# Gathering expert tokens with the hidden state as the stationary operand

## The chip, the cores and the metric

The kernel runs on one core of a Trainium2 chip. The metric is the device time of one execution in microseconds (us), the median of several runs. TensorE is the matmul engine (PE in the profile; PEld is its loading of the stationary operand), VectorE is DVE, ScalarE is ACT, GpSimd is POOL, and SP is the queue that issues the transfers from HBM.

## What is computed

Two layers of a transformer trunk over 256 tokens of width 1024. The second layer's channel mixer is a mixture of experts, and the change lies there:

```python
logits = xf @ w_router                       # 256 x 8
top_logits, top_e = top_k(logits, 2)
gates = softmax(top_logits)
...
y = swiglu(x[rows of expert e], w1[e], w3[e], w2[e])   # for each of 8 experts
out[token] += y[row] * gate[row]
```

All weights are float32; the eight experts alone have 352 MB of them, each read once.

## The kernel before, in words

**Stages.** Layer 0 ends near 410 us of the profiled span, the attention of layer 1 near 570 us, the experts run from about 590 to 1470 us, and the last gate projection closes the kernel. Matrix products with the large experts and dense layers are made of three passes over numbers split in two: `hi` is the value rounded to the chip's single-pass float32 form (float32r, written by ACT), `lo` is the rest (written by DVE). `mm3` (lines 141 to 144) multiplies hi by hi, lo by hi, hi by lo. `split_unit` (lines 93 to 112) splits 1024 columns of weights at a time: `whi` on ACT (line 103), `wlo` on DVE (line 111); five buffers of each.

**Weights.** SP issues transfers of 1 MB into rings of twelve raw buffers (`raw`, `side`, `post`, `early`), in the program's order; a buffer is free again once its weights have been split or, for the small experts, multiplied.

**Router.** `norm_turn` (lines 403 to 428) normalises h, transposes it (line 280), splits the transposed halves (lines 137 and 138) and has the router's matmuls made (lines 460, 461). Then `swiglu_moe` copies the logits (`lgT`, line 997), turns them (line 1000), finds the two best experts of each token (lines 1008, 1009), builds the one-hot choice (lines 1012 to 1017) and each token's slot in its expert's list (lines 1021 to 1025), and counts (line 1028). Lines 1031 to 1033 split h itself, in its natural layout with tokens on the partitions, into `hsh` (ACT, line 137) and `hsl` (DVE, line 138), 128x1024 for each of the two tiles of tokens. `gates()` and `ranks()` (lines 1044 to 1089) make the gate values and sort the experts by their count; line 1088 reads the sorted experts' numbers into SP's registers, and every later transfer of a sorted expert's weights needs them.

**Gather.** For each expert, `gather` (lines 1096 to 1145) builds a one-hot matrix `oh` (tokens x places, line 1103), multiplies it as the stationary operand by hsh and hsl as the moving ones (lines 1116, 1117: eight matmuls of 512 columns, two tiles of tokens, two halves of the width, hi and lo), copies the sums to `xs` (ACT, line 1118), transposes `xs` in eight pieces (line 1131 for a large expert, line 1123 for a small one), and copies or splits the result into the form in which it is a stationary operand itself: `xg_h`, `xg_l` (lines 137, 138) for a large expert, `xe` (line 1124) for a small one. Then `oh` is transposed for the way back (line 1138), and the gate of each row is gathered (line 1140). Five experts have 128 places (large), one 64 and two 32 (small).

**Order.** `STEPS` lists 26 (expert, columns) steps by hand. Expert 0 is gathered first, two steps are done with it, and each other expert is gathered two steps ahead of its first step. Within that, the framework's scheduler orders the instructions of each engine: an instruction traced earlier goes first if it is ready; `tc.issue_after(x)` puts the instructions traced in its block behind x, but only those on x's own engine. In the profiled run the eight gathers begin on PE at 592.0 (expert 0), 609.3 (rank 7, 32 places), 725.2 (rank 1), 890.3 (rank 2), 940.8 (rank 5, 64 places), 1096.7 (rank 3), 1156.1 (rank 6, 32 places) and 1266.2 us (rank 4).

Of the kernel before, what the change touches and what calls it, by code (L numbers as in the profile page):

```python
# [9 lines left out]
FT = mybir.dt.float32  # L10
# [4 lines left out]
AF = mybir.ActivationFunctionType  # L15
# [3 lines left out]
S, D, DEPTH = 256, 1024, 2  # L19
NT = S // 128  # L20
KD = D // 128
N_IN = 2956
D_FF, N_EXP = 3584, 8
# [30 lines left out]
def body(ctx, tc, nc, I, out):  # L54
# [5 lines left out]
    def ps_tile(shape, tag, bufs):  # L60
        return psum.tile(shape, FT, tag=tag, name=tag, bufs=bufs)
# [4 lines left out]
    def work():  # L66
        return ps_tile([128, 512], "wk", 4)
# [22 lines left out]
    last = {}  # L90
# [45 lines left out]
    def split_sb(hi, lo, src):  # L136
        ins = nc.scalar.activation(hi, src, AF.Copy)
        last["lo"] = nc.vector.tensor_sub(lo, src, hi.bitcast(FT))  # L138
        return ins
# [12 lines left out]
    ident = consts.tile([128, 128], FT, name="ident")  # L152
    nc.vector.tensor_scalar(ident, rel, 0.0, None, op0=OP.is_equal)
    h = pers.tile([128, NT, D], FT, name="h")
# [832 lines left out]
    def swiglu_moe(hT, logits, closing):  # L987
        hh, hl = hT
        with tc.tile_pool(name="moe", bufs=1, reuse_waits="tile") as mp:
            hsh = mp.tile([128, NT, D], FR, name="hsh")  # L990
            hsl = mp.tile([128, NT, D], FR, name="hsl")
            sums = pers.tile([128, NT, 2], FT, name="sums", tag="lnsm", bufs=2)
            quarters = mp.tile([128, NT, 4], FT, name="quarters")
            table("exp_and_others", last["sqrt"])
            lgT = mp.tile([128, D], FT, name="lgT", tag="xs", bufs=1)[:2 * N_EXP, :S]
            for t in range(NT):
                nc.vector.tensor_copy(lgT[:, t * 128:(t + 1) * 128], logits[t])
            ps = work()[:, :NT * 2 * N_EXP].rearrange("p (t j e) -> p t j e", t=NT, j=2)
# [31 lines left out]
            done = {}  # L1030
            with tc.issue_after(last["turn"].ins):
                for t in range(NT):
                    done["hs"] = split_sb(hsh[:, t], hsl[:, t], h[:, t])
            xg_h = pers.tile([128, KD, 256], FR, name="xgh", tag="hTh")
            xg_l = pers.tile([128, KD, 256], FR, name="xgl", tag="hTl")

# [59 lines left out]
            def gather(r, n, off, half):  # L1096


                small = n < 128
                sr, gr = (slot, gate) if r == 0 else (slot_r, gate_r)  # L1100
                oh = mp.tile([128, NT, 128], FR, name="oh", tag="oh", bufs=1)
                for t in range(NT):
                    done["oh"] = nc.vector.tensor_scalar(
                        oh[:, t].rearrange("p (j s) -> p j s", s=n),
                        slots[:, None, off:off + n].to_broadcast([128, 128 // n, n]),
                        sr[:, t, r:r + 1], None, op0=OP.is_equal)
                if off == 0 and r == 0:
                    with tc.issue_after(done["oh"].ins):
                        gates()
                        ranks()  # L1110
                xs = mp.tile([128, D], FT, name="xs", tag="xs", bufs=1)
                for f in range(2):
                    fs = slice(f * 512, (f + 1) * 512)
                    p = work()
                    for t in range(NT):
                        nc.tensor.matmul(p, oh[:, t], hsh[:, t, fs], start=t == 0, stop=False)
                        nc.tensor.matmul(p, oh[:, t], hsl[:, t, fs], start=False, stop=t == NT - 1)
                    nc.scalar.activation(xs[:, fs], p, AF.Copy)
                if small:
                    x = mp.tile([128, KD, 64], FT, name="xe", tag="xe", bufs=1)[:, :, :n]  # L1120
                    p = work()[:, :KD * n].rearrange("p (a b) -> p a b", b=n)
                    for k in range(KD):
                        nc.tensor.transpose(p[:, k], xs[:n, k * 128:(k + 1) * 128], ident[:n, :n])
                    nc.scalar.activation(x, p, AF.Copy)
                else:
                    b0 = half * 128
                    x = xg_h[:, :, b0:b0 + 128], xg_l[:, :, b0:b0 + 128]
                    for k0 in range(0, KD, 4):
                        p = work().rearrange("p (a b) -> p a b", a=4)
                        for j in range(4):  # L1130
                            nc.tensor.transpose(p[:, j], xs[:, (k0 + j) * 128:(k0 + j + 1) * 128], ident)
                        ins = split_sb(x[0][:, k0:k0 + 4], x[1][:, k0:k0 + 4], p)
                    if off == 0 and r == 0:
                        table("silu_and_others", ins)
                p = work()
                ohT = mp.tile([128, NT, 128], FR, name="ohT", tag="ohT", bufs=3)
                for t in range(NT):
                    nc.tensor.transpose(p[:, t * 128:(t + 1) * 128], oh[:, t].bitcast(FT), ident)
                for t in range(NT):
                    nc.tensor.matmul(p[:, 256:257], oh[:, t].bitcast(FT), gr[:, t, r:r + 1],  # L1140
                                     start=t == 0, stop=t == NT - 1)
                nc.scalar.activation(ohT, p[:, :256].rearrange("p (t b) -> p t b", t=NT), AF.Copy)
                gs = mp.tile([128, 1], FT, name="gs", tag="gs", bufs=3)
                nc.vector.tensor_copy(gs, p[:, 256:257])
                return x, ohT, gs
# [333 lines left out]
```

## Time and profile before

| | |
|---|---|
| median of 3 runs | 1513.24 us (1512.91 to 1515.36) |
| the profiled execution | 1511.99 us, its span 1510.2 us |
| PE busy | 1421.4 us (94%) |
| weight loads (PEld) | 1054.7 us (70%) |
| DVE busy | 975.8 us (65%) |
| ACT busy | 812.8 us (54%) |
| read from HBM | 454.42 MB, 302 GB/s over the span |

In the timeline a row gives the start in us, the duration in us, the engine, the line, the operation, the result and its inputs, the tile's shape, the number of instructions merged (x4: the duration is then from the first start to the last end), and in brackets the idle time before it with what ended it. A matmul's duration is longer than the distance to the next one, since matmuls are pipelined; the distance from start to start is what one costs. In the table of stretches the columns are the stretch, its length, busy us of each engine with the count of instructions, the granted clock of TensorE as a share of 2.4 GHz, the busy share of the DMA engines, and GB/s.

### The profile page before, as it was taken

Reading aid. Unit: us, or ns where it says so; the run is one execution under the profiler, and the core shown is the slowest. Engines: PE = TensorE matmul, PEld = TensorE weight load, DVE = VectorE, ACT = ScalarE, POOL = GpSimd, SP = SyncE. Lnnn points to the kernel's source line nnn. Section 1 sums busy time; section 2 is a strip of 40 time slices with the busy share of each in tenths; the row PEclk is TensorE's granted clock in tenths of the full one; section 3 lists DMA queues with packets and bytes.
Section 4 is the critical chain, followed back from the end, with each engine's and each line's share of the span. In section 5 each row is a group of like instructions: output and inputs, shape, how many; then the busy total and the mean of one; then the engine's idle time right before and its main releaser. Section 6 shows DMA issues by size and latency. Waiting matters only on the chain. (4 is left out here: it accounts for less than half of the span.)

```text
span 1510.2 us, 19841 instructions
## 1 busy us (share of the span) xinstructions
PE 1421.4 (94%) x7298; PEld 1054.7 (70%) x7298; DVE 975.8 (65%) x1347; ACT 812.8 (54%) x1120; POOL 8.1 (1%) x16
## 2 busy tenths in 40 slices
PE   7999899999999997988999989999899997999968
PEld 6677788888786776746877668853478755777736
DVE  7676654554676767626888568930288854898745
ACT  5466543443555466526766457720277644777534
POOL 0000000000000000000000000000000000000000
PEclk9999999999999998999999999999999999999989
DMA  8643655454346642999999999999999999999893
GB/s 282 221 153 133 223 185 205 167 192 171 99 150 206 224 154 75 383 419 412 406 413 344 408 405 413 416 382 398 414 407 413 405 408 412 407 413 403 304 362 112
DMA packets 125065, 456.84 MB, mean 303 GB/s; under 512 B 10976, under 2 KB 22048, under 8 KB 103200
## 3 DMA queue, kind: packets, MB, share of 16 engines
q1 hardware_dynamic: 124960, 455.50, 78.2%
q8 instruction: 59, 0.97, 0.3%
q14 instruction: 46, 0.38, 0.1%
HBM read 454.42 MB, written 1.05 MB: 302 GB/s over the span
## 5 line engine op out<-in xcount | busy, mean ns | idle before, releaser
L111 DVE TENSOR_TENSOR wlo<-raw,whi 128x1024 fp32r<-128x1024 f32 (+1 forms) x238 | 282.0, 1214 | 91.4 <-ACT whi L103 86.7
L103 ACT ACTIVATE whi<-raw 128x1024 fp32r<-128x1024 f32 (+1 forms) x238 | 243.1, 1052 | 119.9 <-PE acc L143 54.6
L142 PE MATMUL wk<-whi,xgh 128*128 128x512 f32 x560 | 224.0, 400 | 14.9 <-ACT whi L103 14.9
L143 PE MATMUL wk<-whi,xgl 128*128 128x512 f32 x560 | 221.4, 395 | 0.0
L111 DVE TENSOR_TENSOR wlo<-post,whi 128x1024 fp32r<-128x1024 f32 x132 | 157.6, 1219 | 74.2 <-ACT whi L103 72.4
L144 PE MATMUL wk<-wlo,xgh 128*128 128x512 f32 x560 | 201.8, 399 | 3.0 <-DVE wlo L111 3.0
L103 ACT ACTIVATE whi<-post 128x1024 fp32r<-128x1024 f32 x132 | 135.7, 1056 | 110.8 <-DMA post<-in_moe_w_dram 63.2
L111 DVE TENSOR_TENSOR wlo<-side,whi 128x1024 fp32r<-128x1024 f32 x136 | 162.2, 1218 | 15.5 <-ACT whi L103 9.9
L142 PE MATMUL acc<-whi,gh 128*128 128x512 f32 x392 | 155.1, 396 | 8.9 <-ACT whi L103 7.9
L143 PE MATMUL acc<-whi,gl 128*128 128x512 f32 x392 | 154.3, 394 | 0.0
L103 ACT ACTIVATE whi<-side 128x1024 fp32r<-128x1024 f32 x136 | 139.8, 1056 | 25.7 <-PE acc L143 14.2
L144 PE MATMUL acc<-wlo,gh 128*128 128x512 f32 x392 | 142.8, 395 | 0.5
L142 PEld LDWEIGHTS wk<-whi,xgh 128*128 128x128 f32 x560 | 106.9, 191 | 43.6 <-ACT whi L103 19.9
L144 PEld LDWEIGHTS wk<-wlo,xgh 128*128 128x128 f32 x560 | 105.2, 191 | 29.3 <-DVE wlo L111 7.2
L143 PEld LDWEIGHTS wk<-whi,xgl 128*128 128x128 f32 x560 | 106.9, 191 | 22.3 <-DVE xgl L138 0.2
L1367 DVE SCALAR_TENSOR_TENSOR sl<-sl,gs,wk 128x512 f32<-128x512 f32 (+2 forms) x43 | 30.2, 732 | 140.7 <-PE wk L1240 94.0
L142 PEld LDWEIGHTS acc<-whi,gh 128*128 128x128 f32 x392 | 73.5, 188 | 31.5 <-ACT whi L103 12.8
L142 PE MATMUL wk<-whi,hTh 128*128 128x512 f32 x224 | 88.7, 396 | 2.7 <-ACT whi L103 2.7
L144 PE MATMUL wk<-wlo,hTh 128*128 128x512 f32 x224 | 87.9, 393 | 0.0
L143 PE MATMUL wk<-whi,hTl 128*128 128x512 f32 x224 | 87.8, 392 | 0.0
L144 PEld LDWEIGHTS acc<-wlo,gh 128*128 128x128 f32 x392 | 72.7, 188 | 20.9 <-DVE wlo L111 4.4
L143 PEld LDWEIGHTS acc<-whi,gl 128*128 128x128 f32 x392 | 73.6, 188 | 16.6
(396 smaller groups left out, 2119.4 us busy)
## 6 DMA issues: line engine op xcount, KB each, us to landing
raw<-in_moe_w_dram SPq DMA_DIRECT2D x96, 1024.0 KB, 15.2
side<-in_moe_w_dram SPq DMA_DIRECT2D x75, 1024.0 KB, 15.1
post<-in_moe_w_dram SPq DMA_DIRECT2D x75, 1024.0 KB, 15.6
early<-in_moe_w_dram SPq DMA_DIRECT2D x50, 1024.0 KB, 15.8
raw<-in_ffn_w_dram SPq DMA_DIRECT2D x19, 1024.0 KB, 5.2
raw<-in_w_in_dram SPq DMA_DIRECT2D x15, 1024.0 KB, 7.3
post<-in_ffn_w_dram SPq DMA_DIRECT2D x14, 1024.0 KB, 5.2
raw<-in_moe_w_dram SPq DMA_DIRECT2D x17, 768.0 KB, 6.6
```

What stands on the lines that cost most here:

```text
L103: nc.scalar.activation(hi, v, AF.Copy)
L111: engine.tensor_sub(lo, v, hi.bitcast(FT))
L142: nc.tensor.matmul(ps, xh, wh, start=first, stop=False)
L143: nc.tensor.matmul(ps, xl, wh, start=False, stop=False)
L144: return nc.tensor.matmul(ps, xh, wl, start=False, stop=last)
L1367: nc.vector.scalar_tensor_tensor(sl[:, fs], sl[:, fs], now.gs, p, op0=OP.mult, op1=OP.mult)
```

## The change

The gather's operands change places: a 128-column piece of hsh or hsl is the stationary operand, and the one-hot matrix of 128 (or 64, or 32) columns moves, so that the product comes out transposed. `xs`, its two copies and the eight transposes go. For each four pieces of the width there are sixteen matmuls into one bank of PSUM: hsh and hsl of the first tile of tokens, then of the second. A small expert's `xe` is copied in two halves. `lgT` gets a tile of its own. The split of h is taken apart: both `hsh` stay where they were; `hsl` of the first tile stands behind the last low half that was split before it (`last["lo"]`), and `hsl` of the second tile behind expert 0's one-hot matrix, ahead of `gates()` and `ranks()`. `done["hs"]`, behind which the experts' instructions are put, becomes the DVE instruction of the second `hsl`, where it was the ACT instruction of the second `hsh`.

```diff
-            lgT = mp.tile([128, D], FT, name="lgT", tag="xs", bufs=1)[:2 * N_EXP, :S]
+            lgT = mp.tile([128, S], FT, name="lgT")[:2 * N_EXP]
...
             with tc.issue_after(last["turn"].ins):
                 for t in range(NT):
-                    done["hs"] = split_sb(hsh[:, t], hsl[:, t], h[:, t])
+                    done["hs"] = nc.scalar.activation(hsh[:, t], h[:, t], AF.Copy)
+            with tc.issue_after(last["lo"].ins):
+                nc.vector.tensor_sub(hsl[:, 0], h[:, 0], hsh[:, 0].bitcast(FT))
...
                 if off == 0 and r == 0:
                     with tc.issue_after(done["oh"].ins):
+                        done["hs"] = nc.vector.tensor_sub(hsl[:, 1], h[:, 1], hsh[:, 1].bitcast(FT))
                         gates()
                         ranks()
-                xs = mp.tile([128, D], FT, name="xs", tag="xs", bufs=1)
-                for f in range(2):
-                    fs = slice(f * 512, (f + 1) * 512)
-                    p = work()
-                    for t in range(NT):
-                        nc.tensor.matmul(p, oh[:, t], hsh[:, t, fs], start=t == 0, stop=False)
-                        nc.tensor.matmul(p, oh[:, t], hsl[:, t, fs], start=False, stop=t == NT - 1)
-                    nc.scalar.activation(xs[:, fs], p, AF.Copy)
                 if small:
                     x = mp.tile([128, KD, 64], FT, name="xe", tag="xe", bufs=1)[:, :, :n]
-                    p = work()[:, :KD * n].rearrange("p (a b) -> p a b", b=n)
-                    for k in range(KD):
-                        nc.tensor.transpose(p[:, k], xs[:n, k * 128:(k + 1) * 128], ident[:n, :n])
-                    nc.scalar.activation(x, p, AF.Copy)
                 else:
                     b0 = half * 128
                     x = xg_h[:, :, b0:b0 + 128], xg_l[:, :, b0:b0 + 128]
-                    for k0 in range(0, KD, 4):
-                        p = work().rearrange("p (a b) -> p a b", a=4)
+                for k0 in range(0, KD, 4):
+                    p = work()[:, :4 * n].rearrange("p (a b) -> p a b", a=4)
+                    for v, (hs, t) in enumerate(((hsh, 0), (hsl, 0), (hsh, 1), (hsl, 1))):
                         for j in range(4):
-                            nc.tensor.transpose(p[:, j], xs[:, (k0 + j) * 128:(k0 + j + 1) * 128], ident)
+                            nc.tensor.matmul(p[:, j], hs[:, t, (k0 + j) * 128:(k0 + j + 1) * 128], oh[:, t, :n],
+                                             start=(v, j) == (0, 0), stop=v == 3, skip_group_check=True)
+                    if small:
+                        nc.scalar.activation(x[:, k0:k0 + 4], p, AF.Copy)
+                    else:
                         ins = split_sb(x[0][:, k0:k0 + 4], x[1][:, k0:k0 + 4], p)
+                if not small:
```

## Rows read from the trace of the kernel before

**Rows 1.** The profiled page: DMA share by fortieths of the span; one costly group.
```profile
DMA  8643655454346642999999999999999999999893
...
L103 ACT ACTIVATE whi<-raw 128x1024 fp32r<-128x1024 f32 (+1 forms) x238 | 243.1, 1052 | 119.9 <-PE acc L143 54.6
```

**Rows 2.** The table of stretches, seven stretches of the experts' stage.
```profile
590.00:597.00 7.00, 5.31 (x20) 4.14 (x21) 5.83 (x26) 3.01 (x6) 0.00 (x0) 0.50 0.00 1
...
633.00:639.00 6.00, 6.00 (x34) 4.12 (x36) 0.13 (x1) 0.00 (x0) 0.00 (x0) 1.00 0.77 313
...
674.00:687.00 13.00, 5.93 (x81) 2.06 (x73) 0.07 (x1) 1.16 (x2) 0.00 (x0) 0.85 1.01 414
...
796.00:832.00 36.00, 35.99 (x179) 28.00 (x182) 29.51 (x29) 23.72 (x27) 0.00 (x0) 1.00 0.94 334
...
986.00:993.00 7.00, 7.00 (x35) 3.41 (x35) 1.41 (x2) 0.44 (x1) 0.00 (x0) 1.00 0.71 268
...
1180.00:1210.00 30.00, 30.00 (x151) 22.47 (x154) 23.30 (x24) 16.28 (x19) 0.00 (x0) 1.00 1.00 400
...
1402.00:1420.00 18.00, 17.45 (x78) 13.47 (x77) 14.18 (x15) 11.24 (x14) 0.00 (x0) 1.00 0.69 237
```

**Rows 3.** The waits of SP's own queue, 560 to 645 us: us in total, times, longest.
```profile
SPq L1088 <- DVE ids L1065: 26.7, 1, 26.7
```

**Rows 4.** The timeline of DVE, 587 to 596.5 us, around the router's small steps.
```profile
587.59 1.22 DVE L138 TENSOR_TENSOR hsl<-h,hsh 128x1024 fp32r<-128x1024 f32 x1
...
588.88 1.21 DVE L138 TENSOR_TENSOR hsl<-h,hsh 128x1024 fp32r<-128x1024 f32 x1
590.00 0.08 DVE L1009 MATCH_VALUE_LOAD i<-m,lg 128x8 f32 x1
...
591.55 0.48 DVE L1103 TENSOR_SCALAR oh<-slots,slot 128x128 fp32r<-128x128 f32 x2
...
596.15 0.16 DVE L1065 FIND_INDEX8 ids<-top,key 128x8 uint32<-128x8 f32 x1
```

**Rows 5.** The timeline of PE, the first gather (expert 0): its first matmul, and what follows its transposes.
```profile
591.99 0.77 PE L1116 MATMUL wk<-hsh,oh 128*128 128x512 f32 x1 [0.63 <-DVE oh L1103]
...
597.34 0.60 PE L1138 MATMUL wk<-ident,oh 128*128 128x128 f32 x2
```

**Rows 6.** The timeline of PE, a large expert's gather (rank 2).
```profile
890.33 0.39 PE L1116 MATMUL wk<-hsh,oh 128*128 128x512 f32 x1
...
892.20 0.60 PE L1131 MATMUL wk<-ident,xs 128*128 128x128 f32 x4
893.06 0.66 PE L1131 MATMUL wk<-ident,xs 128*128 128x128 f32 x4 [0.25 <-ACT xs L1118]
893.55 0.38 PE L1138 MATMUL wk<-ident,oh 128*128 128x128 f32 x2
```

**Rows 7.** The timeline of PE, a small expert's gather (rank 7).
```profile
609.33 0.39 PE L1116 MATMUL wk<-hsh,oh 128*128 128x512 f32 x1
...
611.66 0.44 PE L1138 MATMUL wk<-ident,oh 128*128 128x128 f32 x2
...
613.17 0.43 PE L1123 MATMUL wk<-ident,xs 32*128 32x32 f32 x4
613.53 0.50 PE L142 MATMUL wk<-whi,xgh 128*128 128x512 f32 x1
```

**Rows 8.** The timeline of PEld: loads of 128 columns that follow one another closely.
```profile
120.01 0.97 PEld L580 LDWEIGHTS wk<-pj,PT 128*128 128x128 f32 x8 [0.26 <-ACT PT L573]
...
613.53 0.19 PEld L142 LDWEIGHTS wk<-whi,xgh 128*128 128x128 f32 x1
613.64 0.19 PEld L143 LDWEIGHTS wk<-whi,xgl 128*128 128x128 f32 x1
```

**Rows 9.** The timeline of PE: the router's matmuls, 16 columns stationary, 128 moving.
```profile
578.63 0.22 PE L460 MATMUL acc<-hTh,rws 128*16 128x128 f32 x1
578.69 0.23 PE L461 MATMUL acc<-hTl,rws 128*16 128x128 f32 x1
```

## The prediction, made before the kernel was run

> **What bounds the kernel.** I read the page's DMA line first: from the fifteenth of the forty slices on, when the experts begin, nearly every digit is 9 [rows 1], so the first thought is that HBM sets the pace and that nothing PE does there matters. The table of stretches corrects this. There are stretches in which the DMA share is over 1.0 and PE is idle for half the time, as from 674 to 687 us [rows 2]; others like it lie around the small experts. But there are also stretches in which PE is full and the DMA engines are short of work: 633 to 639 us at a share of 0.77, 796 to 832 at 0.94, 986 to 993 at 0.71, 1402 to 1420 at 0.69 [rows 2]. There every raw buffer is full, and the next transfer waits until PE has used one up. So the two take turns: a large expert is bound by PE until the transfers stall, a small one by HBM until PE stalls. PE time added ahead of a DMA hole widens the hole and counts in full; PE time added where PE would wait for weights anyway costs nothing.
>
> Ahead of all this stands the router. SP waits 26.7 us in line 1088 for the sorted experts' numbers [rows 3], and DVE makes these with small instructions between which stand large ones: two splits of h of 1.2 us each among them [rows 4]. PE starts expert 0's gather at 591.99 us, at a granted clock of 0.50 in this stretch, the lower of its two levels, 1.2 GHz [rows 2, 5].
>
> **The old gather's cost on PE.** In rank 2's gather the eight 512-column matmuls take 892.20 - 890.33 = 1.87 us, 0.234 us each; the whole takes 893.55 - 890.33 = 3.22 us, since PE also waits 0.25 us for the copy to `xs` [rows 6]. The gathers of ranks 1, 3 and 4 have the running expert's matmuls between their parts, which hides that wait; I price them by 1.87 plus eight transposes at the 893.55 - 893.06 = 0.49 us for four, 2.85 us. Rank 7's, a small one, takes 611.66 - 609.33 = 2.33 us and then 613.53 - 613.17 = 0.36 us for the other four transposes, 2.69 us [rows 7]; ranks 5 and 6 are priced alike.
>
> **The new gather's cost on PE.** It is 32 matmuls of at most 128 moving columns, and each needs another 128-column piece of h loaded. The moving itself would take 0.06 us: that is the distance between the router's matmuls, with 128 moving columns and only 16 stationary [rows 9]. The loads take more. Eight loads of 128 columns with 64 moving ones stand (0.97 - 0.19) / 7 = 0.111 us apart, and the two loads of split operands at 613.53 and 613.64 us stand 0.11 apart [rows 8]. In the old gather 0.234 us of moving covered such a load; here 0.06 doesn't. So 32 x 0.111 = 3.56 us. The ends of this price are 32 x 0.06 = 1.92 us, if loads hid behind the moving, and 32 x (0.111 + 0.06) = 5.5 us, if they stood one behind the other; I take 3.56, because rows 8 have loads of just this shape. Between a running expert's matmuls it is the same: the load that follows a short matmul is as uncovered.
>
> Added on PE, then: rank 7 0.87, rank 1 0.71, rank 2 0.34, rank 5 0.87, rank 4 0.71 us; each has a DMA hole behind it (633, 796, 986 for two of them, 1402). Sum **+3.50 us**. Ranks 3 and 6 (0.71 + 0.87 = 1.58 us) have no hole behind them: from 1180 to 1210 us the share is still 1.00 [rows 2]. I count them at nothing; the cover is HBM's lead over PE, and if it is used up they cost up to 1.58.
>
> The Trainium skill prices this differently: TensorE: Matmul & The Clock Gate, section Back-to-back issue gap, gives about 81 ns a pair as sustained for loads and matmuls of 128 columns. By it the 32 would take 2.59 us, 0.26 less than the old large gather and 0.10 less than the small one, and the whole change would come out near 1510.6 us. Rows 8 speak against it for these float32 loads.
>
> **The first gather.** The second split of h leaves the chain ahead of the one-hot matrix: the next step stood at 590.00, and the split before it began at 588.88 us, so 1.12 us are won [rows 4]. I leave the first split where it is; it has the same inputs and stands as early in the program. The second now stands behind the one-hot matrix and ahead of `gates()` and `ranks()`, 1.21 us there, so the experts' numbers and SP's next transfer come about 0.1 us later; that is covered, since at 633 to 639 us the transfers wait for PE anyway [rows 2]. PE needs the second split for its thirteenth matmul only; at the half clock twelve take over 2.5 us, so that it doesn't wait.
> The old gather took 597.34 - 591.99 = 5.35 us from its first matmul to the end of its transposes [rows 5], at the lower clock. The new one at half clock takes twice 3.56, 7.12 us, 1.77 more; with the clock up after half of it, 5.34, which is the same. With the 1.12 us won: between +0.65 and -1.13 us. I take the middle, **-0.25 us**.
>
> **What else moves.** ACT loses sixteen copies to `xs`; it is busy 54% and ends no wait in these stretches: nothing. The bank count of a gather falls from five to three: nothing that I can price. No transfer and no SP or POOL instruction is added. Since `done["hs"]` is now on DVE, nothing keeps ACT's copies of expert 0's weights behind `hsh`: one of 1.05 us [rows 1] can slip into the normalisation ahead of the router. Bounds 0 and 1.05; I take 0, as ACT has idle time ahead of it in which the free buffers can be filled.
>
> **Sum.** 3.50 - 0.25 = +3.25 us. Against the profiled execution's 1511.99 us that is 1515.2; its time lies 1.25 us under the median of 1513.24, on which the forecast is put: **1516.5 us**. With the first gather's bounds and the ranks 3 and 6: 1515.6 to 1519.1.
>
> **Rivals.**
> *Loads hide (faster).* If loads of h ran under the moving, at 0.06 us a pair [rows 9], the large gathers would fall from 2.85 to 1.92 (-0.93), rank 2's by 1.30, the small ones by 0.77; in all -4.70 us where it counts. The first gather would take 3.84 at half clock, -1.51, and start 1.12 earlier. Together -7.3 us: 1505.9. It turns on one number: below 0.089 us a pair for the large and 0.084 for the small ones the middle gathers gain, above they lose. Against it are rows 8; for it, that only two of those loads are of split operands, and those stand under one long matmul. Chance 0.19, with everything down to the page's distance in it.
> *HBM covers the middle gathers (no change).* The DMA line says 9 nearly throughout [rows 1]; if a wider hole were made up later by transfers that catch up, only the first gather would count: 1512.1 to 1513.9, middle 1513.0. Against it: the holes are followed by stretches at shares over 1.0, with nothing to catch up with. Chance 0.18.
> *The clock stays low (slower still).* The new matmuls use the array about half of the time (0.06 of 0.111 us). If that doesn't lift the clock, the gather costs 7.12 us and expert 0's first matmuls run at half clock as well. PE worked some 5.35 us before the clock had risen; as much again of expert 0's work at half speed loses 2.7. With 3.50 + 0.65 + 2.7 = 6.85: 1520.1, and 1521.7 if ranks 3 and 6 count. Chance 0.16.
> *The change doesn't do what it says.* If the scheduler puts the first split into DVE's wait for the router's last matmuls, another 1.1 us is won, 1515.4; if it puts it where it was, nothing. Both lie in the forecast's case.
>
> **How the numbers follow.** Forecast 0.47, loads hide 0.19, HBM covers 0.18, clock low 0.16. 0.2% is 3.0 us, about what a measurement of this kernel can tell from no change: faster means under 1510.2, slower over 1516.3. The forecast's case lies on this border: 0.28 of its 0.47 over it, 0.19 under. Slower: 0.28 + 0.16 = 0.44. No change: 0.19 + 0.17 + 0.02 = 0.38. Faster: 0.17 + 0.01 = 0.18. The range runs from 1509.5, which leaves out most of the loads' case, to 1521.0, which leaves out the end of the clock's.
>
> **What would show it.** In the profile after: the new matmuls of a middle gather 0.111 us apart (0.06 and I am wrong on the main term); DMA holes wider behind ranks 7, 1, 5 and 4, by the sums above; the one-hot matrix some 1.1 us earlier; the granted clock rising while the first gather still runs; and ranks 3 and 6 opening no hole near 1180 us. The prediction is wrong if the holes don't widen although the gathers take 3.56 us, or if the first gather moves the start of expert 0 by more than 2 us either way.

## The result, and the profile after

The changed kernel takes **1533.64 us** (median of 4 runs, 1527.25 to 1537.61) against 1514.3 of the kernel before: a ratio of **1.0113, 95% interval 1.009 to 1.0136**, and by the medians 19.3 us more. The forecast was 1516.5, its range ended at 1521.0. The profiled execution took 1537.61 us, the longest of the four, with a span of 1535.8 at a mean granted clock of 0.968; before, the span was 1510.2 at 0.979.

The page's DMA line, which answers to [rows 1], still says 9 nearly throughout:

```profile
DMA  8533654544265353899999999899999899999893
```

The new gathers in PE's timeline: rank 7 and rank 2, which answer to [rows 7, 6], then the start and the end of rank 5's.

```profile
611.16 0.51 PE L1123 MATMUL wk<-oh,hsh 128*128 128x32 f32 x4
...
614.65 0.44 PE L1135 MATMUL wk<-ident,oh 128*128 128x128 f32 x2
...
895.31 0.56 PE L1123 MATMUL wk<-oh,hsh 128*128 128x128 f32 x4
...
898.83 0.41 PE L1135 MATMUL wk<-ident,oh 128*128 128x128 f32 x2
...
958.65 0.53 PE L1123 MATMUL wk<-oh,hsh 128*128 128x64 f32 x4
...
961.24 0.80 PE L1123 MATMUL wk<-oh,hsh 128*128 128x64 f32 x4
961.85 1.04 PE L1123 MATMUL wk<-oh,hsl 128*128 128x64 f32 x4
962.70 0.69 PE L1135 MATMUL wk<-ident,oh 128*128 128x128 f32 x2
```

Rank 2's 32 matmuls take 898.83 - 895.31 = 3.52 us and rank 7's 3.49, whether 128 or 32 columns move: the loads set the pace at 0.11 us, as priced. Rank 5's took 962.70 - 958.65 = 4.05, since it slowed down while its last eight ran. PE had not been idle; it stood in the middle of the gather. The table of stretches says why (columns as in [rows 2]):

```profile
589.60:596.60 7.00, 7.00 (x33) 7.00 (x34) 7.00 (x20) 0.80 (x2) 0.00 (x0) 0.50 0.00 1
596.60:603.10 6.50, 6.50 (x20) 5.38 (x19) 5.16 (x12) 3.77 (x5) 0.00 (x0) 0.50 0.37 130
...
899.50:903.40 3.90, 1.48 (x9) 1.06 (x8) 3.90 (x7) 0.50 (x2) 0.00 (x0) 1.00 1.00 404
903.50:910.30 6.80, 6.43 (x20) 4.99 (x21) 4.44 (x20) 1.23 (x2) 0.00 (x0) 0.50 1.04 396
958.70:961.50 2.80, 2.80 (x28) 2.80 (x26) 2.80 (x4) 0.95 (x2) 0.00 (x0) 1.00 1.02 405
961.50:968.30 6.80, 6.80 (x24) 5.84 (x24) 4.44 (x10) 1.15 (x3) 0.00 (x0) 0.50 1.02 417
968.40:972.00 3.60, 3.60 (x18) 2.95 (x17) 1.92 (x4) 2.17 (x3) 0.00 (x0) 1.00 0.17 68
...
1128.80:1135.60 6.80, 6.80 (x16) 4.82 (x17) 4.75 (x10) 1.06 (x1) 0.00 (x0) 0.50 1.04 394
...
1186.80:1193.60 6.80, 6.80 (x25) 5.93 (x25) 3.08 (x9) 1.99 (x4) 0.00 (x0) 0.50 0.94 379
1193.70:1197.00 3.30, 3.30 (x16) 2.67 (x16) 3.30 (x5) 2.03 (x2) 0.00 (x0) 1.00 0.27 60
```

In the gathers of ranks 5 and 6, and shortly behind those of ranks 2 and 3, the granted clock falls to its lower level, 1.2 GHz, and stays there for 6.8 us, in which PE is full, or nearly (6.43 of 6.80 us behind rank 2), but does half the work: at most 3.4 us each. The price appears one stretch later, where the DMA share drops to 0.17 and 0.27: the transfers have filled the buffers and wait for PE. In the kernel before, the stretches behind the gathers of ranks 2 and 5 were at full clock (rank 6's too), and behind rank 3's, the third row, the lower level lasted 3.4 us ((1 - 0.76) x 7.00 x 2) instead of 6.8:

```profile
897.50:904.30 6.80, 6.80 (x35) 5.74 (x34) 6.80 (x14) 5.07 (x6) 0.00 (x0) 1.00 1.04 390
...
943.50:950.30 6.80, 6.80 (x33) 5.34 (x31) 4.57 (x6) 3.25 (x5) 0.00 (x0) 1.00 1.00 413
1110.00:1117.00 7.00, 6.32 (x21) 4.32 (x22) 6.86 (x14) 4.61 (x6) 0.00 (x0) 0.76 1.00 408
```

Behind ranks 2 and 3 something else stands ahead of the fall. From 899.50 to 903.40 PE worked 1.48 of 3.90 us. The waits of PE in the changed kernel, 715 to 1320 us (us in total, times, longest), then DVE's timeline at rank 2 in the changed kernel, and that of the kernel before:

```profile
PE wk L1176 <- DVE gs L1141: 3.0, 2, 1.7
...
PE wk L1293 <- DVE h L1302: 2.1, 1, 2.1
...
PE wk L1293 <- DVE gs L1141: 1.5, 1, 1.5
PE wk L1293 <- DVE xgl L138: 1.4, 1, 1.4
```

```profile
896.37 2.36 DVE L111 TENSOR_TENSOR wlo<-raw,whi 128x1024 fp32r<-128x1024 f32 x2
898.64 2.35 DVE L111 TENSOR_TENSOR wlo<-side,whi 128x1024 fp32r<-128x1024 f32 x2
900.92 0.68 DVE L138 TENSOR_TENSOR xgl<-wk,xgh 128x512 fp32r<-128x512 f32 x1
...
903.64 0.15 DVE L1141 COPY gs<-wk 128x1 f32<-128x1 f32 x1
```

```profile
891.40 2.35 DVE L111 TENSOR_TENSOR wlo<-raw,whi 128x1024 fp32r<-128x1024 f32 x2
893.67 0.68 DVE L138 TENSOR_TENSOR xgl<-wk,xgh 128x512 fp32r<-128x512 f32 x1
```

The copies that free the gather's PSUM banks (`xgl`, `gs`) now stand on DVE behind four splits of the next weights, where it was two. The order of each engine is fixed when the program is built, and the changed gather got another one. So the trace offers two suspects, the clock and the banks; the third is the first gather, which ran at 0.50 throughout and left the clock low until 603.1 us.

The router's part came out as predicted: `oh` no longer waits for the second split, which now begins right behind it [rows 4].

```profile
589.13 0.48 DVE L1105 TENSOR_SCALAR oh<-slots,slot 128x128 fp32r<-128x128 f32 x2
589.52 1.22 DVE L1111 TENSOR_TENSOR hsl<-h,hsh 128x1024 fp32r<-128x1024 f32 x1
```

### The profile page after: what moved, and what is told of

The parts are those of the page before. It is cut to its first block, busy times and chain, and to the rows that moved or that the text cites. A ratio compares the mean times of both kernels' runs of the same rounds, so it can differ in the third digit from the quotient of the medians.

```text
span 1535.8 us, 20123 instructions
## 1 busy us (share of the span) xinstructions
PE 1444.0 (94%) x7426; PEld 1082.0 (70%) x7426; DVE 983.3 (64%) x1347; ACT 812.2 (53%) x1107; POOL 8.1 (1%) x16
## 5 line engine op out<-in xcount | busy, mean ns | idle before, releaser
L142 PE MATMUL wk<-whi,xgh 128*128 128x512 f32 x560 | 229.7, 410 | 14.3 <-ACT whi L103 14.3
L143 PE MATMUL wk<-whi,xgl 128*128 128x512 f32 x560 | 225.3, 402 | 0.0
L144 PE MATMUL wk<-wlo,xgh 128*128 128x512 f32 x560 | 211.2, 406 | 3.3 <-DVE wlo L111 3.3
L142 PEld LDWEIGHTS wk<-whi,xgh 128*128 128x128 f32 x560 | 109.8, 196 | 45.0 <-ACT whi L103 19.3
## 6 DMA issues: line engine op xcount, KB each, us to landing
early<-in_moe_w_dram SPq DMA_DIRECT2D x50, 1024.0 KB, 13.6
```

The lines of the kernel that those rows point to most:

```text
L142: nc.tensor.matmul(ps, xh, wh, start=first, stop=False)
L143: nc.tensor.matmul(ps, xl, wh, start=False, stop=False)
L144: return nc.tensor.matmul(ps, xh, wl, start=False, stop=last)
```

## The experiments

**The splits alone.** The kernel before with the new places of the splits and the old gather.

```diff
-                    done["hs"] = split_sb(hsh[:, t], hsl[:, t], h[:, t])
+                    done["hs"] = nc.scalar.activation(hsh[:, t], h[:, t], AF.Copy)
+            with tc.issue_after(last["lo"].ins):
+                nc.vector.tensor_sub(hsl[:, 0], h[:, 0], hsh[:, 0].bitcast(FT))
...
+                        done["hs"] = nc.vector.tensor_sub(hsl[:, 1], h[:, 1], hsh[:, 1].bitcast(FT))
```

> The kernel before with the splits of h placed as in the change, and the old gather. Theory A (the new matmuls, which use the array half of the time, bring the granted clock down): the first gather starts about 1.1 us earlier, the clock is low in the same stretches as before, and the time is about 1.0 us under before, 1513.3. Theory B (the cost comes from the new places of the splits, by the order that they give ACT and DVE around the router): at least 5 us over before, 1519 or more.

Measured: 1514.88 us, ratio 1.0011 (0.9998 to 1.0025): nothing gained. Yet the step itself happened. In PE's timelines, from the start of h's last transposes (line 280) to the first gather's first matmul and to rank 7's gather, the kernel before and this one:

```profile
582.76 1.29 PE L280 MATMUL wk<-ident,h 128*128 128x128 f32 x8 [2.93 <-DVE h L400]
```

```profile
583.15 1.29 PE L280 MATMUL wk<-ident,h 128*128 128x128 f32 x8 [2.93 <-DVE h L400]
...
591.30 0.77 PE L1119 MATMUL wk<-hsh,oh 128*128 128x512 f32 x1 [0.63 <-DVE oh L1105]
...
608.79 0.39 PE L1119 MATMUL wk<-hsh,oh 128*128 128x512 f32 x1
```

Before, 591.99 - 582.76 = 9.23 and 609.33 - 582.76 = 26.57 us [rows 5, 7]; here 8.15 and 25.64. So 1.08 us are won at the first gather and 0.93 are left at rank 7's; from there to rank 1's gather this kernel takes 116.55 us against 115.85, and the gain is nearly spent. Behind rank 7's gather lies the stretch in which PE waits for HBM at a share of 1.01 [rows 2]; to come there early most likely buys nothing, though no run tested this by itself.

**The gather alone.** The changed kernel with the splits put back where they were (the diff above, reversed).

> The changed kernel with the splits of h where they were before. Theory A: as slow as the change or about 1 us slower, 1528 to 1537; the granted clock falls during or right after most of the gathers. Theory B: close to before, 1514 to 1517.

Measured: 1536.29 us, ratio 1.0148 (1.0116 to 1.0179). The whole loss is the new gather's.

**More moving columns.** The changed kernel, but every matmul of a gather moves 256 columns, the one-hot matrix and 128 columns of zeros, which add nothing to the sums.

```diff
...
-                            nc.tensor.matmul(p[:, j], hs[:, t, (k0 + j) * 128:(k0 + j + 1) * 128], oh[:, t, :n],
+                            c0, o0 = (j * 128, 128) if j < 3 else (256, 0)
+                            nc.tensor.matmul(bank[:, c0:c0 + 256], hs[:, t, (k0 + j) * 128:(k0 + j + 1) * 128],
+                                             wide[:, t, o0:o0 + 256],
...
```

> The changed kernel with the same 32 loads a gather, but 256 moving columns in each matmul, the one-hot matrix and as many zeros, so that the array is used nearly all of the time that a load takes. Theory A: a middle gather still takes 3.6 to 3.9 us, but the clock stays at 1.00 after the gathers at 958 and 1184 us of the changed kernel, and the time falls to 1515 to 1520. Theory C (the time is lost to the pace of the loads itself and to waits for PSUM banks behind DVE, not to the clock): 1528 or more, as the matmuls are no faster.

Measured: **1517.0 us**, ratio 1.0012 (0.9995 to 1.0028). More work on PE, and 16.6 us less than the changed kernel. Rank 5's gather and the stretches at the first gather, behind rank 5 and behind rank 2:

```profile
949.00 0.66 PE L1127 MATMUL wk<-oh,hsh 128*128 128x256 f32 x4
...
952.84 0.38 PE L1140 MATMUL wk<-ident,oh 128*128 128x128 f32 x2
```

```profile
582.30:592.50 10.20, 6.15 (x40) 5.19 (x39) 7.72 (x27) 3.93 (x6) 0.00 (x0) 0.50 0.01 2
...
952.80:959.60 6.80, 6.80 (x33) 5.25 (x32) 6.80 (x14) 4.26 (x6) 0.00 (x0) 1.00 1.04 417
...
895.00:901.80 6.80, 6.16 (x45) 5.25 (x44) 6.80 (x23) 4.75 (x7) 0.00 (x0) 1.00 1.02 390
```

A gather is longer (952.84 - 949.00 = 3.84 us), but no fall follows it, and at the first gather the clock is up by 592.6, in the middle of the gather, where the changed kernel had it at 603.1. This kernel also has another order on DVE and one wait for a bank, of 0.6 us, so the clock and the banks are not yet apart.

**The old gather, made longer.** The kernel before with four of the eight 512-column matmuls of each gather made twice, 4 x 0.234 = 0.94 us more of PE at full use; what they sum is too large.

```diff
-                    for t in range(NT):
+                    for t in [*range(NT)] * (2 - f):
...
```

> The kernel before with the first four 512-column matmuls of each gather made twice: 0.94 us of PE time added to each gather, at full use of the array. By the prediction's sum (added PE time counts in full at ranks 7, 1, 2, 5 and 4) 4.7 us, and at half clock 1.9 more in the first gather: 1521, and up to 1.9 more if ranks 3 and 6 count. If HBM covers the middle gathers: 1516. If any PE time added there is punished beyond its own length: over 1526.

Measured: 1524.98 us, ratio 1.0074 (1.0055 to 1.0092), 10.8 more than before, above what was expected. Eight gathers at 0.94 are 7.5 us, and those of ranks 3 and 6 count too: counted from h's last transposes to the same matmuls of line 142 in both traces, the delay against the kernel before grows from 11.8 to 13.1 us across rank 6's gather, where no fall lies. In the profiled execution, the longest of the four, the clock took 3.4 us more at most: the stretch at the lower level behind rank 3 lasts 6.8 us instead of 3.4, and one of 3.4 us is new behind rank 2. So a fall can come with 512 columns moving, too. Over the four executions the clock took no more than before (the table below). Of the 3.3 us beyond the 7.5, the first gather at half clock is another 0.94, and PE's wait for the copy to `xs` has grown (at rank 2 from 0.25 to 0.74 us); the remainder is open.

**128 columns for the small experts.** The changed kernel; ranks 5, 6 and 7 move 128 columns, copies of their own.

```diff
...
-                            nc.tensor.matmul(p[:, j], hs[:, t, (k0 + j) * 128:(k0 + j + 1) * 128], oh[:, t, :n],
+                            nc.tensor.matmul(p[:, j], hs[:, t, (k0 + j) * 128:(k0 + j + 1) * 128], oh[:, t],
...
```

> The changed kernel, but the gathers of the three small experts (ranks 7, 5, 6) move 128 columns of the one-hot matrix past each weight load, where they moved 32 or 64; the added columns repeat the expert's own and are not copied out. Theory (a gather that moves few columns per load brings TensorE's granted clock to its lower level): the clock stays at 1.00 in the gathers of ranks 5 and 6 and behind them, which gives back about 3.4 us each of what the changed kernel lost; the falls behind ranks 2 and 3, which follow waits for PSUM, stay. About 1533.6 - 6.8 = 1527 us. Rival (the loads' own pace or the waits bring the clock down, and the number of moving columns does not matter): no change, 1533 to 1535 us, with the clock at 0.50 after ranks 5 and 6 as before.

Measured: 1529.61 us (1527.91 to 1530.71), ratio 1.0099 (1.0072 to 1.0126), 4.0 us less than the changed kernel where 6.8 were expected, and inside the spread of that kernel's executions. Behind ranks 5 and 6 the clock holds (the first two rows), behind ranks 2 and 3 it falls as before:

```profile
962.50:969.30 6.80, 6.80 (x34) 5.66 (x33) 5.51 (x14) 3.14 (x5) 0.00 (x0) 1.00 0.80 331
...
1184.00:1190.80 6.80, 6.57 (x32) 4.99 (x31) 5.96 (x14) 2.72 (x4) 0.00 (x0) 1.00 1.03 417
902.50:909.20 6.70, 5.28 (x19) 4.21 (x20) 5.48 (x23) 0.36 (x1) 0.00 (x0) 0.50 1.04 396
1124.40:1131.10 6.70, 5.63 (x13) 3.97 (x14) 4.82 (x13) 1.06 (x1) 0.00 (x0) 0.50 1.02 391
```

**The banks freed in time.** The changed kernel; the splits of the next step's first weights are issued behind the gather's last copy.

```diff
...
-                nc.vector.tensor_copy(gs, p[:, 256:257])
+                fresh[:] = [nc.vector.tensor_copy(gs, p[:, 256:257])]
...
+                    with ExitStack() as late:
+                        if fresh and base == 0 and s > 1:
+                            late.enter_context(tc.issue_after(fresh[0].ins))
+                        fresh.clear()
+                        ps = now.up("moe_w1", c, turn_last)
```

> The changed kernel, but the splits of the next expert step's first weights are issued after the gather's last copy (gs), so that no gather's PSUM bank stands on VectorE behind the running expert's weight splits. Theory (TensorE's waits for those banks, 8.08 us in the changed kernel against 1.69 before, are a loss of their own and bring the clock down behind ranks 2 and 3): the waits behind ranks 1, 2, 3 and 4 fall to under 2 us in sum, the clock stays at 1.00 behind ranks 2 and 3, and the falls in the gathers of ranks 5 and 6 stay; 1533.6 - 6.4 - 4 = about 1523 us. Rival (the waits are covered by what comes later, and the clock falls by the gather's own pattern): the waits go and the time stays at 1531 to 1535 us, with the clock at 0.50 behind ranks 2 and 3.

Measured: 1531.13 us, ratio 1.0095 (1.0063 to 1.0127). **By the time alone my theory of the banks got no support; the next run shows that half of it holds.** The waits listed above shrank, though not as far as expected: 3.0 + 2.1 + 1.5 + 1.4 = 8.0 us became 3.7, in which two waits of 1.4 at other places are new. Behind rank 2, 1.4 and 1.5 us became one of 0.59; yet the clock fell there all the same, from 900.7 us on, and the time is within the spread of the changed kernel's. Within this kernel's own five executions the time follows the clock: the longest, 1535.45 us, had 0.965, the shortest, 1522.6, 0.972; (0.972 - 0.965) x 1535 = 10.7 of the 12.9 us between them.

**Both together.** 128 columns everywhere, and the banks freed in time: the last two diffs in one kernel.

> Both of the last two edits together: 128 moving columns in every gather, and the next weight splits issued after the gather's last copy. Theory (few columns per load, and waits for PSUM behind VectorE, are all that the change costs beyond the loads): no clock fall in the middle gathers, and the time near that of the kernel with 256 moving columns, 1517 us (1515 to 1520). Rival (128 columns past each load are also too few, and the clock falls in the large experts' gathers too): falls of some 6.8 us at the lower level stay behind ranks 2, 3 or 4, and the time stays above 1524 us.

Measured: 1523.88 us (1522.60 to 1525.83), ratio 1.0065 (1.0043 to 1.0087). **Against the run with 128 columns for the small experts, which differs by the order alone, that is 5.7 us less, and no execution of the one reaches into the other's range.** So the waits for banks do cost time of their own; they are about 7.7 us in that run (3.0, 2.1, 1.4, 1.0 and 0.2) and 4.7 here. The clock explains little of it: over all executions it took 6.1 us more than before there and 4.8 here (the table below).

Yet the time is not down to 1517: the fall behind rank 3 stayed (1119.7, 6.8 us), and the first gather left the clock low until 604.3. But the fall behind rank 2 is gone, and this pair of runs is worth a look, for in both kernels rank 2's gather and what follows are the same instructions. Behind the gather, first the kernel with the order alone, then this one:

```profile
900.73 0.59 PE L1294 MATMUL wk<-yh,ohT 32*128 32x256 f32 x2 [0.59 <-DVE gs L1142]
```

```profile
900.70:907.50 6.80, 6.78 (x25) 5.46 (x26) 6.80 (x22) 1.46 (x3) 0.00 (x0) 0.50 1.03 391
```

```profile
902.13 0.39 PE L1294 MATMUL wk<-yh,ohT 32*128 32x256 f32 x2 [0.59 <-DVE gs L1142]
```

```profile
900.20:907.00 6.80, 5.87 (x39) 4.25 (x39) 6.10 (x23) 2.17 (x4) 0.00 (x0) 1.00 1.02 399
```

The same wait of 0.59 us, the same gather of 3.52 before it: one fell, one held. So such a gather makes a fall possible, and something outside these instructions decides. The gather-alone run says it too: its rank 5, 64 columns at 958.66, took 3.49 us and held, where the changed kernel's, at 958.65, fell.

```profile
962.20:969.00 6.80, 6.80 (x35) 5.69 (x35) 5.75 (x14) 3.06 (x5) 0.00 (x0) 1.00 1.00 408
```

The Trainium skill, TensorE: Matmul & The Clock Gate, section Part 1: The HAM clock gate, says of a start from idle that the number of matmuls at the lower clock differs between runs of one kernel, because the chip's watch on the engine runs on its own and doesn't start with the kernel. No run here shows whether that is also the reason in the middle of work, as in this pair.

**The first gather alone.** The new gather for expert 0, with the new places of the splits; the other seven as before.

```diff
+                if off == 0 and r == 0:
+                    for k0 in range(0, KD, 4):
...
+                else:
+                    xs = mp.tile([128, D], FT, name="xs", tag="xs", bufs=1)
...
```

> The new gather at the first expert alone, with the changed kernel's places of the splits; the other seven experts gather as before. Theory (the new gather does not bring the clock up as the old one did: it stood at 0.50 until 603.1 in the changed kernel against 597.8 before, and the 256-column version brought it up by 592.5): the clock comes up some 5 us later than before, which costs about 2.6 us less the 1.06 won by the earlier start, so about 1516 us, and no fall of the clock behind the other experts. Rival (the prediction's step: the first gather gains 0.25 and the rest is as before): about 1514 us, with the clock up by 598.

Measured: 1520.09 us, ratio 1.004 (1.0028 to 1.0053): **6.7 us for one gather**, more than the theory's 2.6 less 1.06.

```profile
584.10:604.60 20.50, 16.52 (x76) 14.52 (x75) 17.18 (x49) 8.07 (x12) 0.00 (x0) 0.50 0.12 41
```

```profile
583.02 1.38 PE L280 MATMUL wk<-ident,h 128*128 128x128 f32 x8 [2.94 <-DVE h L400]
...
612.73 0.39 PE L1139 MATMUL wk<-hsh,oh 128*128 128x512 f32 x1
```

From h's last transposes to rank 7's gather it takes 612.73 - 583.02 = 29.71 us against 26.57, so 3.14 of the 6.7 are lost there, the 1.08 won included. The other 3.6 come later, where the gathers are the old ones; the trace has two stretches at the lower level there that the kernel before had not (843.5, 3.4 us; 1270.2, 6.8 us). Over its six executions the clock took 5.0 us more than before, and all else 0.2 (the table below), so this part, too, can be the clock; why it fell behind old gathers is open.

**256 columns for the large experts alone.** Ranks 0 to 4 as in the run with 256 columns, the small ones as in the changed kernel.

```diff
+                            if small:
+                                nc.tensor.matmul(p[:, j], hs[:, t, (k0 + j) * 128:(k0 + j + 1) * 128], oh[:, t, :n],
+                                                 start=(v, j) == (0, 0), stop=v == 3, skip_group_check=True)
+                                continue
```

> The changed kernel, but only the large experts' gathers (ranks 0 to 4) move 256 columns, half of them zeros; the small ones move their 32 or 64 as in the changed kernel. Theory (every gather that moves few columns past its loads can bring the clock down, the small ones first): the falls in the gathers of ranks 5 and 6 stay, at 3.4 us each, and those behind ranks 2, 3 and 4 and the long cold stretch at the first gather go; 1517 + 7 = about 1524 us. Rival (what the clock does is set by where a gather lies among the other work, and one gather's columns do not settle it): falls behind ranks 2 or 3 stay, 1528 us or more.

Measured: 1519.5 us, ratio 1.0031 (1.0002 to 1.006), 4.5 under my expectation. The large gathers lose their falls (two stretches of 3.4 us begin with the first pieces of ranks 3 and 4, at 1101.0 and 1271.7 us, behind stretches in which PE was busy for 2.22 of 4.00 and 1.86 of 3.70 us), but so do those of ranks 5 and 6, which still move 64 and 32 columns: rank 5's held, as in the gather-alone run, and rank 6's has the running expert's matmuls between its parts here. Behind rank 7's, with 32 columns, the clock fell instead, after 3.90 us in which PE was busy throughout:

```profile
612.90:616.30 3.40, 3.40 (x10) 2.62 (x9) 1.82 (x5) 1.76 (x3) 0.00 (x0) 0.50 1.01 417
```

That the small gathers always cost 3.4 us is wrong; and where the two falls vanished in the run with 128 columns for them, chance may have had a part.

**A version that may beat both.** The loads are what the new gather pays for, so let two experts share them: ranks 7 and 1, 2 and 5, 3 and 6 are gathered together, both one-hot matrices (256 useful columns) moving past each of the 32 loads; ranks 0 and 4 alone. The splits are issued behind the last copy.

```diff
-                            nc.tensor.matmul(p[:, j], hs[:, t, (k0 + j) * 128:(k0 + j + 1) * 128], oh[:, t, :n],
+                            nc.tensor.matmul(p[:, j], hs[:, t, (k0 + j) * 128:(k0 + j + 1) * 128], oh2[:, t, :wide],
...
+                pairs = {7: 1, 2: 5, 3: 6} if base == 0 else {}
```

> A version that may beat both: the gathers of two experts share their 32 weight loads, with both one-hot matrices (256 columns, all of use) moving past each load. Ranks 7 and 1 are gathered together, 2 and 5, 3 and 6; ranks 0 and 4 alone with 128 columns. The splits are issued after the last copy, as in the run with that order. Theory: a pair takes 32 x 0.120 = 3.85 us at full clock, three pairs 11.6 and rank 4 3.6, together 15.1 us, against 2.69 + 2.85 + 3.22 + 2.69 + 2.85 + 2.69 + 2.85 = 19.8 us in the kernel before; as TensorE is the bound there, 1514.3 - 4.7 = about 1509.6 us. Rival (a longer gather at one place loses the cover that two places had, or its eight copies out of PSUM hold TensorE up): 1514 us or more, with waits for PSUM inside the pairs' gathers.

Measured: 1511.91 us, ratio **0.9982** (0.997 to 0.9995). Faster than both, by less than worked out. Ranks 2 and 5 together:

```profile
891.78 0.41 PE L1130 MATMUL wk<-oh,hsh 128*128 128x256 f32 x2
...
895.63 0.38 PE L1146 MATMUL wk<-ident,oh 128*128 128x128 f32 x2
```

```profile
589.60:603.20 13.60, 12.46 (x53) 11.58 (x54) 12.38 (x35) 4.12 (x6) 0.00 (x0) 0.50 0.09 21
```

The pair took 3.85 us as worked out, but at the first gather, with 128 columns, the clock was again low until 603.2. Two more kernels tried to win that back. In the first, ranks 0 and 4 also move 256 columns, their own matrix twice:

```diff
-                step = 4 // len(parts)
+                step = 2
...
+                        w = 256 // len(parts)
```

> The kernel with paired gathers, but ranks 0 and 4, which are gathered alone, also move 256 columns (their one-hot matrix twice, the second copy not copied out). Theory: the clock comes up at the first gather some 7 us earlier than with 128 columns, and does not fall behind rank 4, for 0.3 us more of TensorE in each: 1511.9 - 3 = about 1509 us. Rival (the paired kernel's falls do not depend on the lone gathers): 1512 us, as without the edit.

Measured: 1511.88 us, ratio 0.9984 (0.9975 to 0.9993). The clock was up by 597.8, 5.4 us earlier, and the time did not change: the rival held. In the second, ranks 0 and 4 go back to the old gather:

```diff
+                if also is None:
+                    xs = mp.tile([128, D], FT, name="xs", tag="gh")
...
```

> The kernel with paired gathers, but the two experts gathered alone (ranks 0 and 4) go back to the old form, one-hot matrix held and 512 columns of h moving, then transposes; its staging tile takes the place of the gate tile. The first expert keeps the changed kernel's places of the splits. Theory (a gather that moves few columns keeps the clock down at the first expert, which by the run with the new first gather alone cost 6.7 us against before): the first gather is as before, so some 4 us come off the paired kernel: 1507 to 1509 us, with the clock up by 598. Rival (in the paired kernel the first gather's clock does not matter, as with the 256-column form of it, which changed nothing): 1511 to 1513 us.

Measured: 1511.21 us, ratio **0.9974** (0.9961 to 0.9987). The clock was up by 595.5, and the time is again the rival's. The three paired kernels are one result, 0.2% under the kernel before. In the first of them 5.8 us are saved outside the clock, where 4.7 were worked out, and the clock takes up to 3.0 back (the table below); the other two save 3.4 and 4.2.

## Why the prediction was wrong

The granted clock sums it up, and over all executions rather than over the profiled ones, since the falls differ between executions. For each kernel: how many executions there are, their mean span over the 1512.7 us of the kernel before (69 executions beside the experiments), how much more the lower clock took, (1 - clock) x span less the 36.3 us of before, and the rest. The clock's part is an upper bound, for some of that time PE was idle. Each number is uncertain by 1 to 2 us.

```
                         executions   span   by the clock, at most   rest
changed kernel                4       18.6          10.0              8.5
splits alone                 10        0.7          -1.8              2.4
gather alone                  4       21.0          14.7              6.3
256 moving columns           10        2.4          -4.6              7.0
old gather made longer        4       10.7          -0.9             11.5
128 columns for the small     4       15.0           6.1              8.8
banks freed in time           5       15.6          13.2              2.4
128 columns, banks freed      5        9.4           4.8              4.6
first gather alone            6        5.2           5.0              0.2
256 columns for the large     5        4.4          -0.2              4.6
pairs                        10       -2.8           3.0             -5.8
pairs, ranks 0 and 4 wide    11       -3.2           0.2             -3.4
pairs, ranks 0 and 4 old     12       -3.3           0.9             -4.2
```

So the change has two costs of about one size. Up to 10.0 of the 18.6 us are the clock's; 256 moving columns bring it back, while the rest, with longer gathers and fewer waits, stays nearly the same (8.5 to 7.0). And 8.5 are not the clock's: where PE only had more to do, as in the old gather made longer, all of the loss stands there, and freeing the banks takes 6.1 us off it in the changed kernel and 4.2 with 128 columns for the small.

*The old gather's and the new gather's price: right.* 0.11 us a load, 3.49 to 3.52 us where 3.56 was said; between a running expert's matmuls, counting from each of the 32 to the next matmul, it is 3.2 to 3.35. The 81 ns a pair of the Trainium skill (TensorE: Matmul & The Clock Gate, section Back-to-back issue gap) are not the pace of these float32 loads: the trace has 0.11 us.

*The rival "loads hide": excluded by the same rows.*

*Ranks 3 and 6 at nothing: wrong.* I reasoned that HBM's lead covers them because no hole lay behind them. The old gather made longer counts all eight. With them the PE term is 0.80 for each small one, 0.30 for ranks 1 and 2, 0.36 and 0.50 for ranks 3 and 4: 3.9 us, not far from the 3.50 said, one error covering another.

*The first gather, -0.25: wrong.* The split's part, 1.08 of 1.12, was right. But I took the middle between a clock that rises midway and one that doesn't, where the step needed a decision. It didn't rise: the changed kernel takes 611.16 - 581.40 = 29.76 us from h's last transposes to rank 7's gather against 26.57, **+3.19**. The third rival had priced just this, 0.65 + 2.7 = 3.35.

```profile
581.40 1.29 PE L280 MATMUL wk<-ident,h 128*128 128x128 f32 x8 [2.94 <-DVE h L400]
```

*The sum: the main step that failed* is that it priced the seven middle gathers at full clock, since PE was busy around them. "The clock stays low" had the cause, columns that move for 0.06 of each 0.11 us, and its chance was 0.16; but I applied it to the first gather alone, where the clock was low already. In the profiled execution, the longest of the four, three falls are new, at ranks 2, 5 and 6, at 3.4 us each, and the one behind rank 3 lasts 3.4 us longer than before, 1.7: 11.9 in all. (At rank 4 the lower level lasts 3.4 us longer too, up to 1.7, but it begins at 1285.8 us, ahead of that gather's first matmul at 1288.6.) From h's last transposes to the end that execution is (1535.8 - 581.40) - (1510.2 - 582.76) = 27.0 us longer. With 3.9 and 3.2 the falls explain 19.0 of them; the rest is about what PE's waits for banks grew by, 6.3 us (8.0 against 1.7), and the 1.7 at rank 4.

*The banks at nothing: wrong.* I saw that a gather uses three banks instead of five and wrote that I could price nothing there. I did not ask where the copies that free these banks would come to stand. They stood behind four splits on DVE, and the two pairs of runs with and without that order show 4.2 and 6.1 us for it outside the clock.

A slip of the sum: the upper end of 1519.1 adds up to 1519.0 (3.50 + 0.65 + 1.58 over 1513.24).

*The rival "HBM covers the middle gathers": wrong.* Where ranks 5 and 6 lose time, the transfers don't catch up: they stop, at a share of 0.17 and 0.27.

**What is shown and what is not.** That the new gather and not the splits costs the time: shown, by the two halves of the change. That more moving columns past the same loads bring nearly all of it back: shown (1533.6 to 1517.0). That this works by the clock rests on these things: with them the lower clock took up to 14.6 us less, and the rest, though it holds fewer waits for banks too, changed by 1.5; the time follows the granted clock between executions of one kernel; and the falls go with the columns over all fourteen traces. In the seven traces whose first gather moves 128 columns past each load the clock came up 12.2 to 13.6 us after that gather's first matmul, in the seven others (256 columns, or the old gather) after 3.0 to 6.2 us. Among the gathers behind it, a fall begins inside the gather (from 0.5 us after its first matmul) or in the 7 us behind its last one at 8 of 12 with 32 or 64 columns, 11 of 27 with 128, and 6 of 50 with 256 or 512, a pair counted as one. That the waits for banks cost time of their own, some 4 to 6 us, is shown by the run with 128 columns and the one with the order added to it; in the changed kernel itself the clock of those executions hid the gain. Which gathers fall in a given execution is not settled; the same instructions did both.

## What to carry to other kernels

Making the narrow operand the moving one turns a matmul that is bound by its moving columns into one bound by its loads: count loads, at the distance that the trace shows. Where few columns move past each load, as the 32 to 128 here, price the granted clock too, not only at the start but in the middle of full work, as something that happens in some executions, and judge it over many executions, not by one trace; where loads must be many, let two users share them, so that more columns move past each. Look where the copies that free PSUM have come to stand in the new order of their engine. And a step won ahead of a stretch that is bound by HBM is not yet time won.

## What was not expected of the hardware

The granted clock fell from 1.00 to 0.50 at 961.5 us with PE busy for every one of the 2.80 us before, in a run of matmuls with 64 columns moving past loads 0.11 us apart; with 256 columns past the same loads it held. Doubling the moving columns from 128 to 256 cost little: 3.84 us a gather against 3.52, since the load covers most of it. And the same instructions, rank 2's gather and the 0.59 us wait behind it, kept the clock in one kernel's execution and lost it in another's.
